# A feed-forward of eight block products per block pair rewritten as two phases over matrix quarters with seven

## The chip, the cores and the metric

The kernel runs on one core of one Trainium2 chip. The metric is the device time of an execution in microseconds (us). The engines are named as in the profile: PE is TensorE, DVE VectorE, ACT ScalarE, POOL GpSimd, SP SyncE, which here only issues transfers.

## The reference

One layer over 1024 tokens of 1024 values, in fp32. Four branches mix the tokens and end in `w_out`; the feed-forward with a hidden width of 4096 follows. Only its end matters here:

```python
hl = hl + ml[2] * yl                                   # yl = (sum of gated branches) @ w_out
bl = modulate(rms_norm(hl, norm_g[i, 1]), ml[3], ml[4])
hl = hl + ml[5] * jnp.square(jax.nn.relu(bl @ w1)) @ w2
return rms_norm(hl, final_g)
```

## The kernel before

Activations lie transposed in SBUF: 128 values by tokens, eight such rows `k` or `d` of values, and two halves of 512 tokens. To keep fp32 accuracy every operand of a large product is split in two: `split` (L72) lets ACT copy it to a rounded high part and DVE subtract that from the original for the low part. `mm3` (L76) then makes three matmuls of 128x512 for a block: high by high, low by high, high by low.

In the stage before, w_out, `hl` is made for each half and row `d` from 24 matmuls, an eviction by DVE that adds the input, ACT's square and POOL's sum of squares (`sum_sq`, L221). At the end of a half the sums are taken by PE against ones, and `second_norm` (L1356) makes the reciprocal root in twelve small DVE steps, broadcasts it by PE (`bcast_rows`, L254) and writes the two parts `blh`, `bll` of the normalised tokens.

The feed-forward runs over 16 blocks of 256 hidden values. For each, `ff1` (L1397) makes the hidden values of one half of the tokens: 8 rows x 3 matmuls for each of two 128-wide chunks, ReLU and square on ACT, and a split into `hh` and `hlw`. `ff2` (L1425) multiplies them by the block's two rows of `w_ff2` and adds each of the eight results to `hl` on DVE. Weights come in transfers of 512 KB on SP's queue (`load_w`, `load_chunk`) and are split in halves of 1024. The second half's `second_norm` is a generator that is advanced between the first block's products. `last_norm` (L1435) takes the final norm into the last block, the second half of tokens in two pieces of 256. The order on each engine is made by a scheduler from the program order and the buffers.

## Time and profile before

| | us |
|---|---|
| median of three runs (lowest, highest) | 1675.32 (1674.51, 1675.99) |
| the profiled execution | 1672.36 |
| its span, first to last instruction | 1670.6 |
| PE busy | 1636.5 (98%) |
| DVE, ACT, POOL busy | 935.9, 552.0, 185.7 |

The span is what one profiled execution of the core shows; 1.76 us of its own time lie around it. Busy time of an engine says how full it is, not what waits for it.

### The profile page before, as it was taken

The page shows a single profiled execution, that of the slowest core. Times are in us where ns is not written, and L with a number is a line of the kernel's source. Part 1 is how long each engine was busy: PE and PEld are TensorE (multiplying, and loading weights), DVE is VectorE, ACT ScalarE, POOL GpSimd, SP SyncE. Part 2 cuts the span into 40 slices and gives each one's busy share as a digit, 9 for nine tenths or more (in the row PEclk, how much of TensorE's full clock was granted, in tenths as well). Part 3 has the DMA queues.
Part 4 walks back from the last instruction along what each step waited for, and adds up shares of the span by engine and source line. Part 5 has one row for each costly group of instructions (what it writes and reads, how often), then busy time and mean ns, then how long its engine had stood idle before and what let it go on. Part 6 is the DMA issues. An engine that isn't in the chain of part 4 may idle for free.

```text
span 1670.6 us, 21735 instructions
## 1 busy us (share of the span) xinstructions
PE 1636.5 (98%) x8464; PEld 1352.7 (81%) x8464; DVE 935.9 (56%) x1913; ACT 552.0 (33%) x897; POOL 185.7 (11%) x281
## 2 busy tenths in 40 slices
PE   8999999999999999999999999999999999999996
PEld 7787878887787787788888888888888888888885
DVE  5797787966556736744446554444444444444455
ACT  3433123222246535623233432222222222222234
POOL 2311102113211212110012200000000000000003
PEclk7999999999999999999999999999999999999997
DMA  8332204425322333143334311111111111111102
GB/s 301 117 99 75 59 27 139 122 86 172 130 86 89 130 107 116 69 157 96 96 109 133 124 51 51 51 51 51 43 46 51 51 51 51 51 51 51 39 1 101
DMA packets 59703, 145.27 MB, mean 87 GB/s; under 512 B 15953, under 2 KB 23713, under 8 KB 59601
## 3 DMA queue, kind: packets, MB, share of 16 engines
q1 hardware_dynamic: 35264, 93.09, 16.7%
q0 software_dynamic: 14688, 47.69, 9.0%
q10 hardware_dynamic: 9648, 3.12, 0.8%
q8 instruction: 66, 1.08, 0.3%
q14 instruction: 37, 0.30, 0.1%
HBM read 126.33 MB, written 17.53 MB: 86 GB/s over the span
## 4 chain that ended last, share of the span: by engine, by line
PE 87%; DVE 6%; DMA 2%; ACT 2%; issue 2%; POOL 0%; SPq 0%; DVEq 0%; ACTq 0%; POOLq 0%
PE mm L77 25%; PE mm L78 25%; PE mm L79 25%; PE po L1189 2%; PE pt L1172 1%; DMA x<-in_xT 1%; PE sc L1146 1%; PE sc L1147 1%; PE mm L736 0%; PE mm L738 0%; PE mm L737 0%; DVE wlo L63 0%; PE pn L235 0%; DMA mraw<-in_ada 0%; PE pt L1176 0%
## 5 line engine op out<-in xcount | busy, mean ns | idle before, releaser
L77 PE MATMUL mm<-alh,whi 128*128 128x512 f32 x704 | 280.1, 398 | 0.4 <-DVE gsg L63 0.4
L79 PE MATMUL mm<-alh,wlo 128*128 128x512 f32 x704 | 276.7, 393 | 0.0
L78 PE MATMUL mm<-all,whi 128*128 128x512 f32 x704 | 276.6, 393 | 0.0
L70 DVE SCALAR_TENSOR_TENSOR hl<-mm,modl,hl 128x512 f32<-128x512 f32 (+1 forms) x264 | 189.9, 732 | 102.9 <-PE mm L79 102.8
L78 PE MATMUL mm<-hlw,w2h 128*128 128x512 f32 (+1 forms) x528 | 202.6, 384 | 1.7 <-DVE hlw L63 1.7
L79 PE MATMUL mm<-hh,w2l 128*128 128x512 f32 (+1 forms) x528 | 202.8, 385 | 0.0
L63 DVE TENSOR_TENSOR wlo<-raw,whi 128x1024 fp32r<-128x1024 f32 x92 | 112.9, 1228 | 159.1 <-ACT whi L73 158.9
L77 PE MATMUL mm<-hh,w2h 128*128 128x512 f32 (+1 forms) x528 | 201.6, 385 | 0.0
L78 PE MATMUL mm<-bll,whi 128*128 128x512 f32 x512 | 199.8, 390 | 0.0
L77 PE MATMUL mm<-blh,whi 128*128 128x512 f32 x512 | 199.6, 390 | 0.0
L79 PE MATMUL mm<-blh,wlo 128*128 128x512 f32 x512 | 199.5, 390 | 0.0
L73 ACT ACTIVATE whi<-raw 128x1024 fp32r<-128x1024 f32 x92 | 97.3, 1059 | 261.2 <-PE mm L78 249.8
L77 PEld LDWEIGHTS mm<-alh,whi 128*128 128x128 f32 x704 | 132.4, 188 | 28.6 <-issue 2.6
L79 PEld LDWEIGHTS mm<-alh,wlo 128*128 128x128 f32 x704 | 132.5, 188 | 27.9 <-issue 1.2
L78 PEld LDWEIGHTS mm<-all,whi 128*128 128x128 f32 x704 | 132.6, 188 | 27.0 <-issue 1.5
L63 DVE TENSOR_TENSOR hlw<-r,hh 128x512 fp32r<-128x512 f32 x64 | 48.3, 754 | 169.3 <-ACT hh L73 169.3
L78 PEld LDWEIGHTS mm<-hlw,w2h 128*128 128x128 f32 x528 | 99.9, 189 | 22.0 <-DVE hlw L63 2.3
L73 ACT ACTIVATE w2h<-raw 128x1024 fp32r<-128x1024 f32 x32 | 33.9, 1059 | 252.6 <-PE mm L78 250.9
L77 PEld LDWEIGHTS mm<-hh,w2h 128*128 128x128 f32 x528 | 99.4, 189 | 20.4 <-ACT hh L73 1.3
L79 PEld LDWEIGHTS mm<-hh,w2l 128*128 128x128 f32 x528 | 99.9, 189 | 19.5
L77 PEld LDWEIGHTS mm<-blh,whi 128*128 128x128 f32 x512 | 96.1, 188 | 20.1
L79 PEld LDWEIGHTS mm<-blh,wlo 128*128 128x128 f32 x512 | 96.1, 188 | 19.9
(448 smaller groups left out, 2575.0 us busy)
## 6 DMA issues: line engine op xcount, KB each, us to landing
raw<-in_w_ff SPq DMA_DIRECT2D x64, 512.0 KB, 3.3
raw<-in_w_in SPq DMA_DIRECT2D x52, 512.0 KB, 3.6
mraw<-in_ada POOLq DMA_DIRECT2D x64, 256.0 KB, 3.4
pmd<-pm POOLq DMA_DIRECT2D x16, 512.0 KB, 3.7
pm<-pmd POOLq DMA_DIRECT2D x16, 512.0 KB, 3.9
raw<-in_w_out SPq DMA_DIRECT2D x16, 512.0 KB, 3.7
ad<-in_ada SPq DMA_DIRECT2D x10, 512.0 KB, 8.4
x<-in_xT SPq DMA_DIRECT2D x8, 512.0 KB, 7.2
```

What stands on the lines that cost most here:

```text
L63: V.tensor_tensor(out=o, in0=x, in1=y, op=op)
L70: V.scalar_tensor_tensor(out=o, in0=x, scalar=s, in1=y, op0=op0, op1=op1)
L73: S.activation(hi, src, AF.Copy)
L77: T.matmul(acc, w[0], x[0], start=start, stop=False)
L78: T.matmul(acc, w[0], x[1], start=False, stop=False)
L79: T.matmul(acc, w[1], x[0], start=False, stop=stop)
L1146: T.matmul(o, q1[h][:, qs], kk, start=True, stop=False)
L1147: T.matmul(o, q2z[h], kk, start=False, stop=True)
L1172: T.transpose(pa[:, b * 128 : (b + 1) * 128], e[:, b * 128 : (b + 1) * 128], ident)
L1189: T.matmul(o[64 * h : 64 * h + 64], vtok[:kp, vt, head * 64 : head * 64 + 64], pts[h][:kp, b], start=(b == 0), stop=(b == nblk - 1), tile_ ...
```

## The change

The two matrices of the feed-forward and its tokens are taken in quarters: halves of the inner rows and halves of the tokens or outer rows. A product of two 2x2 block matrices is then made of seven block products of sums and differences of the blocks instead of eight (Strassen's scheme in Winograd's form). A *visit* `u` is one pair of 128-wide output blocks: 16 visits of the first matrix, 16 of the second. In a visit, product `j` (0 to 6) is 12 matmuls of 128x512 between the split weight combination `ah`, `al` and one of seven token operands `xo[j]`, each of a high and a low part of 128x4x512.

- The weights come as quarters of 256 KB (tag `raw`, 6 buffers). POOL makes `s1` to `s4` from them in each visit; every combination that is multiplied is split by ACT and DVE, three products ahead (`LOOK`).
- The products of a visit accumulate in three banks X, Y, Z. `after1` evicts them and makes seven combinations of the hidden values with ACT, DVE and POOL, and writes each to memory (`hopd`, SP's queue). `after2` adds the results of the second matrix to `hl`, four of seven through ACT and POOL, three by DVE.
- Behind visits 15, 19, 23 and 27, `refill` loads the next four rows of each combination from memory and splits them into the same single `xo[j]`: 28 loads, 28 ACT copies, 28 DVE subtractions each time.
- The first eight visits (`PRO`) are divided: their products 0 and 1 come first, sixteen in all, while the second norm ends and `first_operands` builds `xo[2]` to `xo[6]`. What they leave goes through memory (`m1d`, `hopd[0]`), and the five others of each visit come after.
- `hl` goes to memory in the w_out stage (`hld`) and is loaded again at the 17th product. The last norm takes the second half of tokens in one piece.

```diff
-        def ff1(w1, half, more=()):
-            xs = slice(half * 512, half * 512 + 512)
-            hh = fp.tile([128, 2, 512], F32R, tag=f"hh{half}", name=f"hh{half}", bufs=2)
-            hlw = fp.tile([128, 2, 512], F32R, tag=f"hlw{half}", name=f"hlw{half}", bufs=2)
-            for c in range(2):
-                acc = ps_mm()
-                w = w1[c]
-                for k in range(NK):
-                    mm3(acc, (w[0][:, k], w[1][:, k]), (blh[:, k, xs], bll[:, k, xs]), k == 0, k == NK - 1)
-                r = fp.tile([128, 512], F32, tag="r", name="r", bufs=3)
-                S.activation(r, acc, AF.Relu)
-                S.activation(r, r, AF.Square)
-                split(hh[:, c], hlw[:, c], r)
-                if more:
-                    next(more, END)
-                    next(more, END)
-            return hh, hlw
...
+                stt(hl[:, d, xs], acc, modl[0][:, d : d + 1], xin, ALU.mult, ALU.add)
+                nc.sync.dma_start(hld[:, d, xs], hl[:, d, xs])
+                sum_sq(dp, ss, hl[:, d, xs], d, 512, G)
...
+        for u in range(0, PRO, 2):
+            visits((u, u + 1), (0, 1))
+        for u in range(PRO):
+            visits((u,), (2, 3, 4, 5, 6))
+        for u in range(PRO, 28):
+            visits((u,), range(7))
+        for js in ((0, 1, 2, 4, 6), (3, 5)):
+            for u in (28, 30):
+                visits((u, u + 1), js)
+        def fetch(v):
+            if v["raw"] is None:
+                u = v["u"]
+                v["raw"] = []
+                for c in range(1 if v["js"] == (0, 1) else 2):
+                    src = a["w_ff1"][2 * u + c] if u < 16 else a["w_ff2"][u - 16, c]
+                    for k in range(2):
+                        raw = t_("raw", 6)
+                        nc.sync.dma_start(raw, src[:, 512 * k : 512 * k + 512])
+                        v["raw"].append(raw)
...
+        def prep(n):
+            v, j = steps[n]
+            fetch(v)
+            js = v["js"]
+            q11, q12, *rest = v["raw"]
+            if rest and not v["sums"]:
+                q21, q22 = rest
+                s1, s2 = t_("s", 4, "s1"), t_("s", 4, "s2")
+                G.tensor_tensor(out=s1, in0=q21, in1=q22, op=ALU.add)
+                G.tensor_tensor(out=s2, in0=s1, in1=q11, op=ALU.subtract)
+                v["sums"] = {2: s2, 3: s1, 6: q22}
+                if 4 in js:
+                    s3 = v["sums"][4] = t_("s", 4, "s3")
+                    G.tensor_tensor(out=s3, in0=q11, in1=q21, op=ALU.subtract)
+                if 5 in js:
+                    s4 = v["sums"][5] = t_("s", 4, "s4")
+                    G.tensor_tensor(out=s4, in0=q12, in1=s2, op=ALU.subtract)
+            src = q11 if j == 0 else q12 if j == 1 else v["sums"][j]
+            hi = fp.tile([128, 512], F32R, tag="ah", name="ah", bufs=4)
+            lo = fp.tile([128, 512], F32R, tag="al", name="al", bufs=4)
+            split(hi, lo, src)
+            aops[n] = (hi, lo)
...
+        def product(n, bank, first):
+            j = steps[n][1]
+            hi, lo = aops.pop(n)
+            xh, xl = xo[j]
+            for k in range(4):
+                ks = slice(k * 128, k * 128 + 128)
+                T.matmul(bank, hi[:, ks], xh[:, k], start=first and k == 0, stop=False, skip_group_check=True)
+                T.matmul(bank, hi[:, ks], xl[:, k], start=False, stop=False, skip_group_check=True)
+                T.matmul(bank, lo[:, ks], xh[:, k], start=False, stop=k == 3, skip_group_check=True)
...
+        def operand(j, k, src, eng=None):
+            xh, xl = xo[j]
+            S.activation(xh[:, k], src, AF.Copy)
+            (eng or V).tensor_tensor(out=xl[:, k], in0=src, in1=xh[:, k].bitcast(F32), op=ALU.subtract)
...
+        def after1(u, j, c, pro):
+            if j == 0:
+                c["m1"] = t_("m", 5)
+                S.activation(c["m1"], c["Z" if pro else "X"], AF.Copy)
+                if pro:
+                    nc.sync.dma_start(m1d[u], c["m1"])
+            elif j == 1:
+                h = c["h11"] = hid()
+                if pro:
+                    square(h, c["Z"])
+                else:
+                    tt(h, c["Z"], c["m1"], ALU.add)
+                    square_v(h)
+                save(0, u, h)
+            elif j in (2, 4):
+                m = c["u2" if j == 2 else "u3"] = t_("m", 5)
+                if pro:
+                    tt(m, c["X"], c["m1"], ALU.add)
+                else:
+                    S.activation(m, c["X"], AF.Copy)
+                if j == 4:
+                    h = c["h22"] = hid()
+                    G.tensor_tensor(out=h, in0=m, in1=c["m5"], op=ALU.add)
+                    square(h, h)
+                    save(5, u, h)
+            elif j == 3:
+                c["m5"] = t_("m", 5)
+                S.activation(c["m5"], c["Y"], AF.Copy)
+            elif j == 5:
+                h = hid()
+                tt(h, c["Y"], c["u2"], ALU.add)
+                square_v(h)
+                t3 = hid()
+                G.tensor_tensor(out=t3, in0=c["h22"], in1=h, op=ALU.subtract)
+                save(4, u, t3)
+                G.tensor_tensor(out=h, in0=h, in1=c["h11"], op=ALU.subtract)
+                save(3, u, h)
+                t2 = c["t2"] = hid()
+                tt(t2, c["h22"], h, ALU.subtract)
+                save(2, u, t2)
+            else:
+                h = hid()
+                if pro:
+                    tt(h, c["X"], c["m1"], ALU.add)
+                    square_v(h)
+                else:
+                    square(h, c["X"])
+                save(1, u, h)
+                t4 = hid()
+                tt(t4, h, c["t2"], ALU.subtract)
+                save(6, u, t4)
...
+        def after2(u, j, c):
+            d = 2 * (u % 4)
+            s1, s2 = modl[3][:, d : d + 1], modl[3][:, d + 1 : d + 2]
+            o11, o12, o21, o22 = (box["hl"][:, e, xs] for e in (d, d + 1) for xs in (T1s, T2s))
+            def part(bank, s, o, eng=G):
+                m = t_("m", 5)
+                S.activation(m, bank, AF.Copy, scale=s)
+                eng.tensor_tensor(out=o, in0=o, in1=m, op=ALU.add)
+            def whole(bank, s, o):
+                stt(o, bank, s, o, ALU.mult, ALU.add)
+            if j == 0:
+                part(c["X"], s1, o11)
+            elif j == 1:
+                whole(c["Z"], s1, o11)
+                if u >= 28:
+                    norm_part(d, 0)
+            elif j == 2:
+                part(c["X"], s1, o12)
+            elif j == 3:
+                part(c["Y"], s2, o22, V if u >= 28 else G)
...
+        def refill(j, kb):
+            xo[j] = x_op(P_xa if j < 2 else xbp, j)
+            for q in range(4):
+                t = hid()
+                nc.sync.dma_start(t, hopd[j][4 * kb + q])
+                operand(j, q, t)
...
+        LOOK, AHEAD = 3, 8
+        box = {}
+        live = {}
+        norm2 = second_norm(fp, ss, 1)
+        first = first_operands()
+        next(norm2)
+        for n in range(LOOK):
+            prep(n)
+        for n, (v, j) in enumerate(steps):
+            u, pro = v["u"], v["pro"]
+            for w, _ in steps[n : n + AHEAD]:
+                fetch(w)
+            if n + LOOK < len(steps):
+                prep(n + LOOK)
+            if n < 2 * PRO:
+                for g in (norm2, norm2, norm2) if n < 4 else (first,):
+                    next(g, END)
+            elif n == 2 * PRO:
+                for _ in first:
                     pass
-                continue
-            h0 = ff1(w1, 0)
-            if b < NB - 1:
-                h1 = ff1(w1, 1)
-                w2 = ff2_weights(b)
-                for half, h in ((0, h0), (1, h1)):
-                    for _ in ff2(w2, h, half * 512, 512):
-                        pass
+                box["hl"] = P_hl.tile([128, NK, L], F32, tag="hl", name="hl")
+                for d in range(NK):
+                    nc.sync.dma_start(box["hl"][:, d], hld[:, d])
+                S.activation(one, onec, AF.Sqrt)
+            c = live.setdefault(u, {})
+            nxt = steps[n + 1] if n + 1 < len(steps) else (v, j)
+            if u < PRO and j == 2 or n + 1 == 2 * PRO:
+                w = u + 1 if j == 2 else 0
+                if w < PRO:
+                    m = live[w]["m1"] = t_("m", 5, "m1")
+                    nc.sync.dma_start(m, m1d[w])
+            if pro and j == 3:
+                c["h11"] = hid()
+                nc.sync.dma_start(c["h11"], hopd[0][u])
+            bank = "Z" if j == 1 or (pro and j == 0) else "Y" if j in (3, 5) else "X"
+            fresh = j in (0, 3) or (j == 1 and not pro) or (j == 2 and pro)
+            if fresh:
+                c[bank] = ps_mm()
+            product(n, c[bank], fresh)
+            if u < 16:
+                after1(u, j, c, pro)
             else:
-                w2 = ff2_weights(b)
-                last_norm(w2, h0, 0, 512, False)
-                h1 = ff1(w1, 1)
-                last_norm(w2, h1, 512, 256, False)
-                last_norm(w2, h1, 768, 256, True)
+                after2(u, j, c)
+            if u in (15, 19, 23, 27) and j <= 6:
+                refill(j, (u - 15) // 4)
```

On PE, where w_out ends, there was before (`pn` is the bank of sums and broadcasts, `mm` one of products):

```order
L79 MATMUL mm<-mh,wlo 128x512
L235 MATMUL pn<-ones,sqa 128x1 x4
L77 MATMUL mm<-blh,whi 128x512
L78 MATMUL mm<-bll,whi 128x512
L79 MATMUL mm<-blh,wlo 128x512
```

The same place now:

```order
L81 MATMUL mm<-mh,wlo 128x512
L241 MATMUL pn<-ones,sqa 128x1 x4
L241 MATMUL pn<-ones,sq 128x1 x4
L264 MATMUL pn<-dg,ones 128x128 x3
L1491 MATMUL mm<-xh_7710,ah 128x512
L264 MATMUL pn<-dg,ones 128x128
L1492 MATMUL mm<-xl_7711,ah 128x512
```

The second half's remaining sums and its broadcast, which stood among the first products, now stand ahead of them. On POOL nothing stood in the feed-forward before its last norm:

```order
L1384 DMA xin<-in_xT 128x512
L231 TENSOR_TENSOR sqa<-sqa,sq 128x512 x2
L1454 TENSOR_TENSOR hl<-hl,rs 128x2x512 x4
L1454 TENSOR_TENSOR hl<-hl,rs 128x2x256 x5
```

In one of the visits of five products it now has (L1552 makes `h22`, L1563 `t3`, L1565 `h`−`h11`; `s1` to `s4` belong to the visits behind):

```order
L1470 TENSOR_TENSOR s1_9490<-raw_9394,raw_9396 128x512
L1552 TENSOR_TENSOR t_9385<-m_9383,m_9357 128x512
L1471 TENSOR_TENSOR s2_9491<-s1_9490,raw_9390 128x512
L1475 TENSOR_TENSOR s3_9494<-raw_9390,raw_9394 128x512
L1563 TENSOR_TENSOR t_9417<-t_9385,t_9414 128x512
L1565 TENSOR_TENSOR t_9414<-t_9414,t_9342 128x512
L1478 TENSOR_TENSOR s4_9496<-raw_9392,s2_9491 128x512
```

Two weight sums stand between `h22` and what is made from it. On DVE, in a block of the feed-forward, there was before:

```order
L63 TENSOR_TENSOR wlo_9552<-raw_9549,whi_9551 128x1024
L70 SCALAR_TENSOR_TENSOR hl_7697<-mm_9415,modl3_78,hl_7697 128x512
L63 TENSOR_TENSOR w2l_9682<-raw_9679,w2h_9681 128x1024
L63 TENSOR_TENSOR hlw1_9342<-r_9398,hh1_9341 128x512
L70 SCALAR_TENSOR_TENSOR hl_7697<-mm_9423,modl3_78,hl_7697 128x512
```

Now, at the refill behind visit 19 (`al` are splits of weights, `xl0` and `xl1` the low parts of refilled operands):

```order
L65 TENSOR_TENSOR al_11863<-s1_11793,ah_11862 128x512
L65 TENSOR_TENSOR al_11901<-s3_11797,ah_11900 128x512
L1498 TENSOR_TENSOR xl0_11883<-t_11884,xh0_11882 128x512
L1498 TENSOR_TENSOR xl0_11883<-t_11888,xh0_11882 128x512
L1498 TENSOR_TENSOR xl0_11883<-t_11892,xh0_11882 128x512
L1498 TENSOR_TENSOR xl0_11883<-t_11896,xh0_11882 128x512
L72 SCALAR_TENSOR_TENSOR hl_8918<-mm_11904,modl3_78,hl_8918 128x512
L1498 TENSOR_TENSOR xl1_11919<-t_11920,xh1_11918 128x512
```

Four subtractions for each operand now stand between the splits of the weights.

## Rows read from the trace of the kernel before

**Rows 1.** The page: span, busy time by engine, the chain that ended last.

```profile
span 1670.6 us, 21735 instructions
PE 1636.5 (98%) x8464; PEld 1352.7 (81%) x8464; DVE 935.9 (56%) x1913; ACT 552.0 (33%) x897; POOL 185.7 (11%) x281
...
PE 87%; DVE 6%; DMA 2%; ACT 2%; issue 2%; POOL 0%; SPq 0%; DVEq 0%; ACTq 0%; POOLq 0%
```

**Rows 2.** Table of stretches; the first is the feed-forward.

```profile
core 0: us, PE busy (x) PEld busy (x) DVE busy (x) ACT busy (x) POOL busy (x), PEclk, DMA share, GB/s
943.00:1652.40 709.40, 707.42 (x3169) 585.42 (x3169) 328.81 (x450) 205.24 (x309) 9.88 (x4) 1.00 0.15 49
220.00:230.00 10.00, 7.88 (x37) 5.03 (x36) 10.00 (x27) 1.06 (x1) 0.00 (x0) 0.83 0.00 1
...
1000.00:1200.00 200.00, 200.00 (x882) 165.37 (x882) 88.81 (x112) 53.27 (x76) 0.00 (x0) 1.00 0.15 50
1640.00:1645.00 5.00, 4.18 (x24) 4.18 (x25) 4.25 (x11) 3.08 (x9) 0.22 (x1) 0.71 0.32 120
```

**Rows 3.** Timeline where w_out ends: start, duration, engine, line, operation, [idle before].

```profile
942.16 0.95 PE L235 MATMUL pn<-ones,sqa 128*128 128x1 f32 x8
...
942.36 0.75 DVE L70 SCALAR_TENSOR_TENSOR hl<-mm,modl,xin 128x512 f32<-128x512 f32 x1 [3.30 <-PE mm L79]
...
942.97 0.48 PE L77 MATMUL mm<-blh,whi 128*128 128x512 f32 x1
...
944.66 0.62 ACT L229 ACTIVATE sq<-hl 128x512 f32<-128x512 f32 x1
...
946.00 0.95 PE L235 MATMUL pn<-ones,sq 128*128 128x1 f32 x8
...
950.19 0.16 DVE L70 SCALAR_TENSOR_TENSOR rd_y<-rd_q,rd_y 128x4 f32<-128x4 f32 x1
...
950.82 0.68 PE L258 MATMUL pn<-dg,ones 128*128 128x128 f32 x4
```

**Rows 4.** PE's timeline in the last block, 256 tokens wide.

```profile
1640.82 0.38 PE L78 MATMUL mm<-hlw,w2h 128*128 128x256 f32 x1 [1.74 <-DVE hlw L63]
1641.04 0.28 PE L79 MATMUL mm<-hh,w2l 128*128 128x256 f32 x1
1641.16 0.28 PE L78 MATMUL mm<-hlw,w2h 128*128 128x256 f32 x1
...
1642.35 0.42 PE L77 MATMUL mm<-hh,w2h 128*128 128x256 f32 x1
1642.56 0.41 PE L78 MATMUL mm<-hlw,w2h 128*128 128x256 f32 x1
...
1645.53 0.28 PE L77 MATMUL mm<-hh,w2h 128*128 128x256 f32 x1
```

**Rows 5.** POOL's timeline, in w_out and in the last norm.

```profile
911.36 2.05 POOL L231 TENSOR_TENSOR sqa<-sqa,sq 128x512 f32<-128x512 f32 x1
...
917.70 2.08 POOL L231 TENSOR_TENSOR sqa<-sqa,sq 128x512 f32<-128x512 f32 x1
...
923.02 1.39 POOL L231 TENSOR_TENSOR sqa<-sqa,sq 128x512 f32<-128x512 f32 x1
...
1630.34 9.88 POOL L1454 TENSOR_TENSOR hl<-hl,rs 128x1024 f32<-128x1024 f32 x4 [690.13 <-ACT rs L1447]
...
1662.55 1.27 POOL L1454 TENSOR_TENSOR hl<-hl,rs 128x512 f32<-128x512 f32 x1 [3.07 <-ACT rs L1447]
```

**Rows 6.** DVE's timeline at the same places.

```profile
912.18 1.77 DVE L70 SCALAR_TENSOR_TENSOR bll<-t,modl,blh 128x512 fp32r<-128x512 f32 x1
...
917.39 1.22 DVE L63 TENSOR_TENSOR wlo<-raw,whi 128x1024 fp32r<-128x1024 f32 x1
...
1632.76 2.88 DVE L63 TENSOR_TENSOR hlw<-r,hh 128x512 fp32r<-128x512 f32 x1 [3.68 <-ACT hh L73]
1638.21 2.56 DVE L63 TENSOR_TENSOR hlw<-r,hh 128x512 fp32r<-128x512 f32 x1 [2.56 <-ACT hh L73]
```

**Rows 7.** Groups by line and form, DVE and ACT: xcount | busy us, mean ns | idle before.

```profile
L70 DVE SCALAR_TENSOR_TENSOR hl<-mm,modl,hl 128x512 f32<-128x512 f32 x248 | 182.5, 748 | 102.3 <-PE mm L79 102.2
L63 DVE TENSOR_TENSOR hlw<-r,hh 128x512 fp32r<-128x512 f32 x64 | 48.3, 754 | 169.3 <-ACT hh L73 169.3
L63 DVE TENSOR_TENSOR gwl<-raw,gwh 128x512 fp32r<-128x512 f32 x16 | 11.0, 685 | 0.0
...
L73 ACT ACTIVATE hh<-r 128x512 fp32r<-128x512 f32 x64 | 40.5, 632 | 2.0
L1407 ACT ACTIVATE r<-mm 128x512 f32<-128x512 f32 x64 | 37.6, 588 | 138.1 <-PE mm L79 138.1
```

**Rows 8.** Transfers of 256 KB: queue, count, size, median us from issue to landing.

```profile
raw<-in_wbr SPq DMA_DIRECT2D x16, 256.0 KB, 2.7
...
out<-hl SPq DMA_DIRECT2D x7, 256.0 KB, 2.2
```

**Rows 9.** PE's timeline at the end, behind the last product.

```profile
1652.04 0.28 PE L79 MATMUL mm<-hh,w2l 128*128 128x256 f32 x1
...
1657.28 0.99 PE L235 MATMUL pn<-ones,sqa 128*128 128x1 f32 x4 [3.60 <-DVE sqa L231]
```

More of the change, by code (lines that the diff above doesn't have):

```diff
@@ L44 @@
 PI_PARTS = _parts(TWO_PI, (9, 11, 11))
+PRO = 8
 R_CONV = 2
@@ L105, in tile_backbone @@
     ysd = dram.tile([2, 128, 2, 1024], F32, name="ysd")
+    hld = dram.tile([128, NK, L], F32, name="hld")
+    m1d = dram.tile([PRO, 128, 512], F32, name="m1d")
+    hopd = [dram.tile([16, 128, 512], F32, name=f"hop{j}") for j in range(7)]
     def rsqrt_steps(y, v, q):
@@ new lines, in t_, with hid, visits @@
+        def t_(tag, bufs, name=None):
+            return fp.tile([128, 512], F32, tag=tag, name=name or tag, bufs=bufs)
+        def hid():
+            return t_("t", 7)
+        steps = []
+        def visits(us, js):
+            vs = [dict(u=u, js=js, raw=None, sums=None, pro=u < PRO) for u in us]
+            steps.extend((v, j) for j in js for v in vs)
+        for u in range(0, PRO, 2):
+            visits((u, u + 1), (0, 1))
+        for u in range(PRO):
+            visits((u,), (2, 3, 4, 5, 6))
```

170 lines of the change are left out of this document (97 added, 73 removed).

## The prediction

> **What bounds the kernel now.** I read the page first: TensorE (PE) is busy for 98% of the span and holds 87% of the chain that ended last [rows 1]. Then the table of stretches: from the first to the last product of the feed-forward PE is busy 707.42 of 709.40 us at full clock, and in a quiet stretch 882 matmuls take 200.00 us [rows 2], so 0.2268 us each, back to back. Before, the feed-forward is 3024 such matmuls and 96 half as wide (0.12 us apart, [rows 4]): 697.3 us, and 12 us of anything else. VectorE (DVE) is busy 329 us of it, ACT 205, POOL 10 [rows 2]. So only fewer matmuls, or PE waiting, can move the time here, and three engines have room for more work if it comes in time. The weights are fetched and split well ahead.
>
> **What is removed.** 32 visits x 7 products x 12 matmuls = 2688 matmuls of the old shape, in place of the equivalent of 3072: 609.6 us. Against the whole old stretch of 709.3 us (942.97 to 1652.3, [rows 3, 9]) that leaves **99.7 us** to be eaten by waits.
>
> **Prices of what is added.** Every new operation is a 128x512 one. On DVE, a split's subtraction or a combination costs 0.68, an eviction with an addend 0.75; on ACT a copy 0.63, an eviction 0.59 [rows 7]; a 256 KB transfer lands 2.2 to 2.7 us after its issue [rows 8]. On POOL an addition takes 1.27 when alone [rows 5]; with dispatch I use 1.3.
>
> What decides is whether DVE and POOL can work side by side. Two rows say they often cannot: the subtraction hlw<-r,hh, two operands from SBUF, takes 0.75 in the mean [rows 7], but 2.88 and 2.56 us in the two cases that fell under POOL's four multiplications from 1630.34 to 1640.22 [rows 5, 6]. The second one ends 0.55 us after POOL's last. The other way round, POOL's addition at 917.70 takes 2.08: DVE's wlo runs until 918.61, and from there 1.17 us are left. And bll at 912.18 takes 1.77 in place of 0.75 beside POOL's addition of 911.36 to 913.41. So I count the time of such DVE operations and of POOL's in one sum, as if they shared one engine. Evictions from PSUM stay outside it.
>
> The Trainium skill, "SBUF — State Buffer", section "Who interferes with whom", makes this a rule: a DVE instruction with two SBUF inputs and a GpSimd instruction that reads SBUF exclude each other for the whole instruction. It speaks against this change, which gives POOL 7 or 8 additions in a visit. These rows agree, in single meetings; no row here shows a long contest. Applied with no slip at all, it would add 4.5 to the first products and 12.6 to the refills below: 84 in place of 67, and the time 1660; with every meeting free the first rival would hold.
>
> **Start (+5.5).** Before, the first product runs at 942.97, right behind the sums of the last w_out block, and the second norm's remainder (ACT's square at 944.66, sums at 946.00, rsqrt until 950.35, broadcast at 950.82) hides under products [rows 3]. In the changed order PE has both sums and three of four broadcast matmuls ahead of the first product. With ACT freer: eviction to 943.1, square 943.8, sums 944.9, twelve small DVE steps of 0.2 each 947.3, dg and broadcast 948.4. That is 5.4 us; bounds 4 and 9 (with PE slow afterwards).
>
> **First 16 products, 43.5 us (+5).** The port sum is: DVE 16 splits and 24 norm and operand steps with two SBUF inputs (27 us), POOL 12 operand steps and some 8 weight sums (26 us), 53 us in all. About half of the excess of 9.5 can slide behind them. Bounds 0 and 10.
>
> **Eight visits of five products, 13.6 us each (+20).** Port sum: DVE 5 splits, 2 squares, 2 subtractions at 0.68 (6.1), POOL 7 at 1.3 (9.1): 15.2, so at least 1.6 too long if all of it excludes. The loop that closes on itself is longer: eviction of product 4, then on POOL h22, the two sums that its queue puts between, t3 and h−h11, then t2 on DVE and what DVE has in its queue, the eviction of product 2 of the next visit, and product 4, which accumulates into the bank so read. It is 7.4 us of DVE and PE and five POOL steps: 7.4 + 5 x 1.3 = 13.9 without sharing, and 16.3 with some 2.4 us of DVE's splits in POOL's way. I take 2.5 us a visit, nearer to the loop; bounds 0 and 5.
>
> **Eight visits of seven products (+2).** Port sum 7.5 + 9.1 = 16.6 of 19.05 us; room is left. Bounds 0 and 8.
>
> **Four refills (+10, then 8, 8, 8).** In the steady second phase the port sum is 4.8 + 10.4 = 15.2 of 19.05. A refill adds 28 subtractions, 19.0 us, between the last product of an operand and its next, so within two visits (38.1 us): 30.4 + 19.0 = 49.4. If none of it slid, 11.3 us would be lost each time, and 12.7 at the first, where a visit of the first phase stands ahead. POOL's additions to hl can slip by the five buffers m (6.5 us), which gives some back; against that the operands are single, so each load waits for the last product of its operand, then 2.7 us to land, 0.63 and 0.68 to split, behind which the splits for the next products queue on ACT and DVE: walked by hand that alone costs 3.5 a time, and 5 at the first, where the saves stand ahead of the loads on SP. I take 8, and 10 at the first. Bounds 10 and 70 for the four. Outside the refills the second phase loses nothing: POOL's eight additions take 10.4 of 19.05 us, and if that cover failed DVE would have to take them at 0.68 each, still within the visit.
>
> **Rest.** Sums and broadcasts that PE still has: +2. Tail: before, 18.3 us follow the last product (1652.3 to 1670.6), 5.0 of them until the sums at 1657.28, since the squares' additions ran against POOL [rows 9]. After, 0.75 and 0.63 and a little (2.1) stand there; the last multiplications and stores are of 512 tokens, 1.3 longer: −1.6. The saves of hl on SP stand behind each eviction; the next weight load's buffer comes free later than that, so I put them at 0; if they held up the loads, each costs up to 2.2 us [rows 8], which the 24 products of a block (5.4 us) cover.
>
> **Sum.** 5.5 + 5 + 20 + 2 + 34 + 2 − 1.6 = 66.9 of the 99.7: −32.8. The profiled execution took 1672.36 (span 1670.6 and 1.76 around it), so 1639.6; the median of the runs lies 2.96 above that execution: **1642**.
>
> **Rivals.**
> - *The added work is hidden.* For it: DVE has more than half of this stretch idle, and POOL's first addition beside an idle DVE took 1.39 (923.02). Then the visits of five cost 14.35 (+6), the refills the hand walk's 5 + 3 x 3.5, the first products nothing: losses 27.4, time 1603. Against it: the 2.88 and 2.56.
> - *PE's clock drops at the gaps.* A PE idle of 1.74 us before 1640.82 is followed by matmuls 0.21 apart in place of 0.12 from 1642.35 until 1645.53 [rows 4], at a granted clock of 0.71 over that stretch, and a 2.1 us idle at 220 goes with 0.83 [rows 2]; so such a gap costs about 1.7 us more. Smaller gaps do not show it. If all 8 visits of five, two gaps per refill and three at the start are of that size: 19 x 1.7 = 32, time 1675, no change.
> - *Slower: refills in series.* The loads use t, of which there are seven; a refill takes four, so the next one's loads wait for its subtractions. One refill alone is 2.7 + 0.63 + 4 x 0.68 + POOL between (1.3) = 7.4 against 2.72 of its product. Were they strictly in series, 7 x 4.7 = 33 less some 8 of prepared products = 25 a time, 100 in place of 34: 1708. It decides from 17 us a refill upwards, where the sum is back at 1675. Against it: nearly two refills fit the seven buffers, and the next use is a whole visit away.
>
> **Chances.** My sum 0.52 (1622 to 1660 by its own bounds), hidden 0.25, clock 0.13, series 0.10. About 3.4 us (0.2%) can be told from no change. The clock's rival straddles it: faster 0.83, same 0.04, slower 0.13. The range reaches from the hidden case to the clock's: 1600 to 1676.
>
> **What would show it.** In the profile after: 2688 products spaced 0.2268 where PE doesn't wait; first product 5 to 6 us behind the last of w_out; visits of five at 15 to 17 us, with PE idle released by an eviction of DVE behind POOL; means of POOL's additions above 1.5 and of DVE's splits above 0.8 where both run, and not elsewhere; visits 16, 20, 24 and 28 later than 19.05 us by 8 to 10 together with the one ahead. I am wrong if POOL and DVE overlap without growing, if PE's idle time is spread over the steady visits, or if waits on SP's queue (a raw that lands late) end most of it.

## The result and the profile after

The changed kernel takes **1692.7 us** (four executions, 1689.13 to 1694.16) against 1674.91 (1673.66 to 1675.99) before: a ratio of 1.0103 [1.0085, 1.0122]. It is slower by 1%, where −2% was predicted. The profiled execution is the slowest of the four (1694.16).

The page of the changed kernel, the lines that answer to [rows 1], and the granted clock in 40 slices:

```profile
span 1692.4 us, 22506 instructions
PE 1600.0 (95%) x8032; PEld 1297.0 (77%) x8032; DVE 1058.2 (63%) x2027; ACT 672.2 (40%) x1147; POOL 557.8 (33%) x533
...
PEclk7999999999999999999999999899999999999997
...
PE 62%; DVE 15%; DMA 8%; issue 7%; ACT 4%; POOL 3%; SPq 0%; DVEq 0%; POOLq 0%; ACTq 0%
```

By the prediction's count PE has 384 full matmuls less, 87 us at the old spacing, and it has lost only 36.5 us of busy time. So those that are left cost more each, even before any wait is counted. PE's part of the chain fell from 87% to 62%.

The table of stretches, in this order: the start; the first 16 products; visits 2 to 6; visits 8 to 14; visits 15 to 17 around the first refill; the last 28 products:

```profile
core 0: us, PE busy (x) PEld busy (x) DVE busy (x) ACT busy (x) POOL busy (x), PEclk, DMA share, GB/s
946.00:953.57 7.57, 3.94 (x23) 3.54 (x22) 3.88 (x19) 3.80 (x6) 0.00 (x0) 0.65 0.65 230
953.57:1009.81 56.24, 48.38 (x196) 37.80 (x196) 44.96 (x51) 32.60 (x59) 26.43 (x17) 0.96 0.52 169
1044.36:1138.00 93.64, 79.85 (x302) 62.66 (x301) 43.96 (x65) 23.59 (x41) 48.76 (x35) 0.89 0.51 168
1156.48:1293.12 136.64, 136.64 (x589) 110.80 (x588) 79.59 (x94) 59.38 (x104) 70.64 (x50) 1.00 0.42 148
1293.12:1365.56 72.44, 63.48 (x254) 48.67 (x253) 54.23 (x63) 37.71 (x68) 38.46 (x26) 0.95 0.65 215
1577.42:1675.46 98.04, 89.29 (x362) 70.94 (x361) 65.82 (x77) 50.80 (x83) 58.91 (x37) 0.91 0.33 109
```

The fourth row is the surprise. Seven visits of 84 matmuls run without one wait and at full clock, yet they take 136.64 us: 19.52 a visit, 0.2324 a matmul, where [rows 2] had 0.2268. The other rows lose through PE's idle time and through the clock. (PE's busy time counts a slowed matmul as busy, so the stretch minus PE's busy time understates the loss.)

What ended PE's waits from 950 to 1680 us (total, times, longest; one of the two in the fifth line lies behind the last product):

```profile
PE mm L1491 <- DVE m L65: 19.5, 7, 3.2
PE mm L1491 <- ACT m L1590: 11.8, 10, 2.8
PE mm L1493 <- DVE al L65: 11.3, 7, 4.4
PE mm L1491 <- ACT m L1533: 7.9, 4, 3.3
PE pn L264 <- DVE dg L69: 4.6, 2, 2.9
...
PE mm L1492 <- DVE xl L1498: 2.2, 3, 0.8
```

The sum of the prediction, term by term. "Measured" is a stretch's time from first product to first product, less its matmuls x 0.2268; the spacing's part is taken out of each and stands in its own line.

| term | predicted | measured |
|---|---|---|
| spacing of the 2688 matmuls | 0 | 15.0 |
| start | 5.5 | 6.8 |
| first 16 products | 5 | 11.6 |
| eight visits of five | 20 | 35.1 |
| visits 8 to 14 | 2 | 0 |
| four refills | 34 (10, 8, 8, 8) | 39.1 (13.9, 6.2, 8.0, 11.0) |
| rest (sums and broadcasts on PE, end) | 2 | 11.2 |
| tail | −1.6 | −1.4 |
| sum | 66.9 | 117.4 |

The last 28 products and visit 27 lose 22.2 together; 11.2 of that is lost without a last refill too (e3 below), which is the line "rest". 117.4 − 99.7 gives +17.7. Another 3.8 of the span's 21.8 lie ahead of the feed-forward, which the sum left out: w_out's last product ends at 946.0, before at 942.2. The longest wait that is new is one near 411 us, in a stage whose operations are the same (changed kernel, then the one before):

```profile
411.41 0.50 PE L79 MATMUL mm<-sg_yh,gwh 128*128 128x512 f32 x1 [3.53 <-ACT gsg L1267]
```

```profile
408.08 0.50 PE L77 MATMUL mm<-sg_yh,gwh 128*128 128x512 f32 x1 [0.46 <-ACT gsg L1261]
```

It is hardly chance: the wait is 2.7 to 3.5 us in all 17 profiles of changed kernels (of the kernel before there is one profile). The change also gives the pool of the weights, which the stages ahead use, another way of handing on its buffers (`reuse_waits="tile"`, L86; the section on the change does not name it). No run tells whether that is the reason. In the kernels below the first product starts anywhere from 950.1 to 955.9. The last 0.3 is rounding and crumbs.

### The profile page after: what moved, and what is told of

The parts are those of the page before. It is cut to its first block, busy times and chain, and to the rows that moved or that the text cites. A ratio compares the mean times of both kernels' runs of the same rounds, so it can differ in the third digit from the quotient of the medians.

```text
span 1692.4 us, 22506 instructions
## 1 busy us (share of the span) xinstructions
PE 1600.0 (95%) x8032; PEld 1297.0 (77%) x8032; DVE 1058.2 (63%) x2027; ACT 672.2 (40%) x1147; POOL 557.8 (33%) x533
## 4 chain that ended last, share of the span: by engine, by line
PE 62%; DVE 15%; DMA 8%; issue 7%; ACT 4%; POOL 3%; SPq 0%; DVEq 0%; POOLq 0%; ACTq 0%
PE mm L79 10%; PE mm L80 10%; PE mm L81 9%; PE mm L1491 8%; PE mm L1492 8%; PE mm L1493 8%; DMA t<-hop 3%; PE po L1195 2%; DVE xl L1498 2%; DMA raw<-in_w_ff 2%; DVE al L65 1%; DMA mraw<-in_ada 1%; ACT xh L1497 1%; PE pt L1178 1%; DVE t L65 1%
## 5 line engine op out<-in xcount | busy, mean ns | idle before, releaser
L1491 PE MATMUL mm<-xh,ah 128*128 128x512 f32 x896 | 365.8, 408 | 42.9 <-DVE m L65 19.5
L1493 PE MATMUL mm<-xh,al 128*128 128x512 f32 x896 | 364.3, 407 | 11.3 <-DVE al L65 11.3
L1492 PE MATMUL mm<-xl,ah 128*128 128x512 f32 x896 | 363.6, 406 | 2.2 <-DVE xl L1498 2.2
L1491 PEld LDWEIGHTS mm<-xh,ah 128*128 128x128 f32 x896 | 175.0, 195 | 94.6 <-issue 17.0
L1493 PEld LDWEIGHTS mm<-xh,al 128*128 128x128 f32 x896 | 174.4, 195 | 56.4 <-DVE al L65 15.3
L1492 PEld LDWEIGHTS mm<-xl,ah 128*128 128x128 f32 x896 | 174.1, 194 | 44.0 <-DVE xl L1498 3.5
L65 DVE TENSOR_TENSOR al<-s,ah 128x512 fp32r<-128x512 f32 x128 | 118.6, 930 | 55.3 <-ACT ah L75 55.3
L65 DVE TENSOR_TENSOR al<-raw,ah 128x512 fp32r<-128x512 f32 x96 | 89.9, 943 | 60.8 <-ACT ah L75 56.6
L1591 POOL TENSOR_TENSOR hl<-hl,m 128x512 f32<-128x512 f32 x60 | 91.5, 1527 | 82.7 <-ACT m L1590 82.4
L1498 DVE TENSOR_TENSOR xl<-t,xh 128x512 fp32r<-128x512 f32 x120 | 105.3, 918 | 7.4 <-ACT xh L1497 7.3
```

The costliest lines, as they stand in the source:

```text
L65: V.tensor_tensor(out=o, in0=x, in1=y, op=op)
L1491: T.matmul(bank, hi[:, ks], xh[:, k], start=first and k == 0, stop=False, skip_group_check=True)
L1492: T.matmul(bank, hi[:, ks], xl[:, k], start=False, stop=False, skip_group_check=True)
L1493: T.matmul(bank, lo[:, ks], xh[:, k], start=False, stop=k == 3, skip_group_check=True)
L1498: (eng or V).tensor_tensor(out=xl[:, k], in0=src, in1=xh[:, k].bitcast(F32), op=ALU.subtract)
L1591: eng.tensor_tensor(out=o, in0=o, in1=m, op=ALU.add)
```

## The experiments

Each ratio is to the kernel before, run beside it on the same chip; "−x" is against 1692.7. The runs were made on several chips, on which the medians of the kernel before lie within 0.9 us. Where no ratio is given, the kernel was run once: executions of one kernel spread over 3 to 17 us, so such a total decides nothing, and the reading rests on the stretches. Diffs are against the changed kernel.

### Why are the matmuls 0.2324 apart?

The form of the instructions differs from the old one in several ways (which operand comes first, which bank accumulates how long, the order of high and low). The rival is the place of the operands in SBUF.

**e1_forms** gives one form each to ten of the visits 9 to 25, and so leaves out or alters part of those products:

```diff
+                if u == 9:
+                    st = k == 0
+                    sk = {}
...
+                elif u == 11:
+                    kk = 0
+                elif u == 12:
+                    ks = slice(0, 128)
+                elif u == 13:
+                    seq = [(hi, xh), (lo, xh), (hi, xl)]
```

> The products of the changed kernel run 0.2324 us apart in undisturbed visits (19.52 us for 84), those of w_out in the same execution 0.2268. Thirteen visits get one altered form each: 9 ends its accumulation group with each product and opens a new one, 10 opens one with each product, 11 always the first rows of the operand, 12 always the first columns of the weights, 13 the order high-low-high of weights, 14 no low weights, 18 no low operand, 21 low by low, 22 a group for each matmul, 25 one pair of operands three times. The parts left out or repeated make the result another one. Theory 1, the spacing comes from what the matmuls read or how they accumulate: one of these visits falls to 0.2268, so 19.05 us. Theory 2, it comes from something outside the matmuls, such as what the other engines and the queues do in this stretch: all stay at 0.232 to 0.234.

1695.39. Every altered visit stays at 232.4 to 233.4 ns a matmul. None of these forms matters.

**f1_low_weights** opens a pool for `ah` and `al` ahead of the token operands, which puts `xo[2]` to `xo[6]` 16 KB higher, and changes nothing else. By the program's allocation the weights then lie at bytes 18144 to 34528 of a partition instead of 112480 to 128864:

```diff
+    P_wt = ExitStack()
+    wtp = P_wt.enter_context(pool("p_wt", reuse_waits="tile"))
...
-            hi = fp.tile([128, 512], F32R, tag="ah", name="ah", bufs=4)
-            lo = fp.tile([128, 512], F32R, tag="al", name="al", bufs=4)
+            hi = wtp.tile([128, 512], F32R, tag="ah", name="ah", bufs=4)
+            lo = wtp.tile([128, 512], F32R, tag="al", name="al", bufs=4)
```

> The split weights ah and al lie at the low end of SBUF (addresses 18144 to 34528 of a partition) in place of 112480 to 128864, the operands xo[2] to xo[6] 16 KB higher; nothing else is changed. The altered forms of the products left their spacing at 0.2324, so neither accumulation nor which rows they read sets it. Theory 1, where the weights lie does (before, all weights lay below 89856): undisturbed visits fall from 19.52 to 19.05 us and the kernel is 12 to 15 us faster. Theory 2, it is something else in this stretch: 19.52, no difference.

1684.35, ratio 1.0056 [1.0034, 1.0078], −8.3. The same 130 us of undisturbed visits, first in the changed kernel, then with low weights:

```profile
1160.00:1290.00 130.00, 130.00 (x561) 105.43 (x560) 77.51 (x90) 56.19 (x98) 66.86 (x47) 1.00 0.43 152
```

```profile
1160.00:1290.00 130.00, 130.00 (x575) 107.64 (x574) 78.39 (x93) 58.97 (x103) 67.80 (x47) 1.00 0.43 154
```

575 matmuls in place of 561, as before the change; an undisturbed visit takes 19.04. About half of the 15 us is kept. Where PE waits for other engines the quicker products gain nothing: the eight visits of five take 146.6 us here and 146.7 in the changed kernel, the first 16 products 56.2 in both.

**i2_ah_low** moves `ah` alone, **i3_alternate** both for every second product (`wp = fp if n % 2 else wtp`):

> Only the high parts ah of the weights lie low (18144 to 26336), al stays high. Theory 1, each weight load from the high place costs its matmul some 17 ns: two of three matmuls are quick, visits of 19.05 + 28 x 0.017 = 19.5 at most, if the slow one alone loses all, or 19.2 if it loses its own share of 5.6 ns a matmul. Theory 2, the operands' place (8 KB higher) did it: 19.05 as with both moved.

> Even products take their weights from the low place, odd ones from the high one; the operands lie 8 KB higher than in the changed kernel for all. Theory 1, the weights' place sets the spacing: 0.2268 in even products, 0.232 to 0.234 in odd ones, after a few matmuls of each. Theory 2, it is the operands' place or the layout as a whole: one spacing for all.

With `ah` low the spacing is 0.2311 in the mean and the total 1687.14. Only the step between the two matmuls that both take `ah` is quick (226.7 ns); the steps on either side of `al`'s matmul take 232.7 and 234.0. Alternating gives 1686.56 and two patterns. The eleven spacings of products 65 (high) and 66 (low), in ns, worked out from the start times:

```
65 high  241 233 230 232 228 230 233 241 232 231 232
66 low   236 224 231 236 228 233 230 227 227 226 227
```

The low product comes down to 227 after some seven matmuls, the high one never does. So the place of the stationary operand (the weights, which PE loads ahead of each matmul) sets the spacing, within one kernel and one stretch. Why its start is slow, and at which address the border lies, stays open.

### What closes the loop of the visits of five?

The prediction's loop went from the eviction of product 4 through POOL and DVE back to product 4. The trace of the changed kernel shows the same end, but another link (visits 5 and 6; start, duration, engine, line):

```profile
1108.02 1.65 POOL L1478 TENSOR_TENSOR s<-raw,s 128x512 f32<-128x512 f32 x1 [2.00 <-DVE al L65]
...
1109.29 0.77 PE L1491 MATMUL mm<-xh,ah 128*128 128x512 f32 x1 [2.83 <-DVE m L65]
...
1110.14 0.68 DVE L65 TENSOR_TENSOR al<-raw,ah 128x512 fp32r<-128x512 f32 x1
...
1110.24 0.32 SPq L1527 DMA_DIRECT2D hop<-t  x1
...
1110.65 0.89 SPq L1456 DMA_DIRECT2D raw<-in_w_ff  x2
...
1115.15 1.29 POOL L1470 TENSOR_TENSOR s<-raw 128x512 f32<-128x512 f32 x1 [5.49 <-DMA raw<-in_w_ff]
...
1116.40 1.30 POOL L1552 TENSOR_TENSOR t<-m 128x512 f32<-128x512 f32 x1
...
1123.36 1.29 POOL L1565 TENSOR_TENSOR t<-t 128x512 f32<-128x512 f32 x1
...
1124.68 0.69 DVE L65 TENSOR_TENSOR t<-t 128x512 f32<-128x512 f32 x1 [3.81 <-POOL t L1565]
...
1127.09 0.68 DVE L65 TENSOR_TENSOR m<-mm,m 128x512 f32<-128x512 f32 x1
...
1127.92 0.48 PE L1491 MATMUL mm<-xh,ah 128*128 128x512 f32 x1 [3.18 <-DVE m L65]
```

A visit needs four `raw` buffers and there are six. POOL's last weight sum of visit 5, `s4` (L1478), has done with a quarter at 1109.67. SP issues the load into its buffer at 1110.65, behind the save at 1110.24, as the first of two; the second goes into the buffer that the split at 1110.14 frees. POOL's first sum of the next visit starts when the first load has landed, 4.5 us after the issue, and has then waited 5.49 us, with h22 (1116.40), the other sums and everything up to DVE's `t2` (1124.68) queued behind. So POOL's own last sum closes the loop, through the buffer and the transfer. Then DVE's eviction of the next visit's product 2 is late, and PE waits 3.18 for the bank. By the order in which the buffers are handed out, a seventh lets this quarter follow the read of `s3` instead, 6 us earlier.

**g1_one_load** leaves the loads of these visits out but for the first one's (visits 1 to 7 use the quarters of visit 0); **h3_raw7** takes one buffer from `t` for `raw`:

```diff
-                        raw = t_("raw", 6)
+                        raw = t_("raw", 7)
...
-            return t_("t", 7)
+            return t_("t", 6)
```

> Left out: the weight loads of visits 1 to 7 for their products 2 to 6; the quarters of visit 0 serve all eight, so the result is another one. Theory 1 (the loop through the weights' buffers and loads): POOL's first sum waits for no load, visits 1 to 6 fall from 18.4 to 16.5 us or less. Theory 2 (POOL's and DVE's sum): they stay at 17.5 or more.

> Seven buffers for raw weight quarters in place of six, six for t in place of seven. Theory 1, the loop of the visits of five runs through the freeing of a raw buffer, the load into it and the first sum: with one buffer more it has one quarter's freedom, visits 1 to 6 fall from 18.4 to 17 us or less (leaving the loads out gave 15.7). Theory 2, all four quarters are freed together too late for one more buffer to matter: 18 or more. The refills, which load into t, lose 1 to 3 us each with one buffer fewer by either.

Both give visits 2 to 7 of 15.70 to 15.76 us, in place of 17.6 to 20.0, with one wait of 1.49 to 1.55 each and the clock at 1.00. Visit 1 gains nothing (19.1 and 20.1 us, for 18.5), and with one buffer fewer for `t` the first products take 59.55 us for 56.24 (59.4 in h4 and i1 below). Totals: 1669.21 and 1678.93. In h3, POOL in the same operations, and PE behind them:

```profile
1058.04 1.30 POOL L1470 TENSOR_TENSOR s<-raw 128x512 f32<-128x512 f32 x1 [1.89 <-DVE al L65]
1059.67 1.61 POOL L1552 TENSOR_TENSOR t<-m 128x512 f32<-128x512 f32 x1 [0.33 <-issue]
1061.24 1.30 POOL L1471 TENSOR_TENSOR s<-s,raw 128x512 f32<-128x512 f32 x1
...
1071.51 0.47 PE L1491 MATMUL mm<-xh,ah 128*128 128x512 f32 x1 [1.50 <-DVE m L65]
```

The first sum no longer waits for a transfer. What is left ends as the loop that the prediction described, at DVE's eviction, and is near its size: 13.6 + 2.5 predicted, 15.7 measured. That it is this loop link by link was not tested.

Two edits were meant for the other links. **e2_pro_act** shortens the eviction of product 2, with ACT's copy freeing the bank and DVE adding `m1` later; **f3_prep_late** writes POOL's sums behind the visit's own additions in the program:

```diff
-                if pro:
+                if pro and j == 4:
...
+                    if pro:
+                        tt(m, m, c["m1"], ALU.add)
```

```diff
+            late = pro and n >= 2 * PRO
+            if n + LOOK < len(steps) and not late:
...
+            if late and n + LOOK < len(steps):
+                prep(n + LOOK)
```

> In the eight visits of five products the bank of product 2 is copied out by ACT, and DVE adds m1 afterwards, off the bank. Theory 1, PE waits before product 4 only because that eviction stands in DVE's queue behind t2, which waits for POOL: the seven waits of 1.8 to 3.2 us and the half clock after each (1.7 us of time each) go, visits fall from 18.5 to 14 us, and the whole kernel is 30 to 35 us faster (about 1660). Theory 2, the sum of POOL's time and DVE's bounds the visits whatever evicts (7 additions of 1.27 and 10 operations of 0.68, 15.7 us): visits stay at 16 or above, with another wait in place of the old, and the gain is 18 us at most.

> In the visits of five products the weight sums and splits of a later product are written behind the product and its eviction, not ahead; POOL's queue then has h22 ahead of s1, and s2, s3 behind t3 and h-h11. Theory 1, the visit's loop runs through the weights (s1 waits for a quarter that is loaded into a buffer which DVE frees late, and h22 stands behind s1 on POOL): visits fall from 18.4 to 15 to 16.5 us, 16 to 25 us faster. Theory 2, it is the sum of POOL's and DVE's time that bounds: order does not matter, 17.5 us or more, under 8 us faster.

e2: 1689.05, ratio 1.0087 [1.0066, 1.0109], −3.6; the wait moves to product 6 (2.11 each) and to `al`, and that gain lies within the noise. f3: 1693.74, 1.0113 [1.0087, 1.0138], visits of 17.1 to 20.2. But f3 did not do what was expected of it: the scheduler put POOL's operations back in the old order, `s1` still ahead of h22 and still waiting for the load.

```profile
1115.13 1.29 POOL L1470 TENSOR_TENSOR s<-raw 128x512 f32<-128x512 f32 x1 [5.50 <-DMA raw<-in_w_ff]
1116.38 1.74 POOL L1552 TENSOR_TENSOR t<-m 128x512 f32<-128x512 f32 x1
1118.08 1.30 POOL L1471 TENSOR_TENSOR s<-s,raw 128x512 f32<-128x512 f32 x1
```

So f3 says nothing on the order. While the load closes the loop, the shorter eviction is worth little; what another order would be worth stays open.

### What makes the refills dear?

**e3_no_refill** leaves the refills behind visits 19, 23 and 27 out (the operands of 15 stay); **e4_no_pool_add** leaves POOL's additions of results to `hl` out (60 in all, four in most visits); **f2_dve_results** gives them to DVE, in one operation from the bank:

```diff
-            if u in (15, 19, 23, 27) and j <= 6:
+            if u == 15 and j <= 6:
```

```diff
-                eng.tensor_tensor(out=o, in0=o, in1=m, op=ALU.add)
+                if eng is V:
+                    V.tensor_tensor(out=o, in0=o, in1=m, op=ALU.add)
```

```diff
-                m = t_("m", 5)
-                S.activation(m, bank, AF.Copy, scale=s)
-                eng.tensor_tensor(out=o, in0=o, in1=m, op=ALU.add)
+                stt(o, bank, s, o, ALU.mult, ALU.add)
```

> Left out: the refills behind visits 19, 23 and 27 (84 loads, copies and subtractions); the operands of visit 16 serve to the end, so the result is another one. Theory 1, the refills cost what visits 19, 20, 23, 24, 27 and 28/29 lost (6, 8 and some 11 us with the half clock): 22 to 27 us faster, the waits on al and on ACT's m gone there, and only the wait before the last products left. Theory 2, these waits come from the steady work of the visits and the pairing of the last four: under 10 us.

> Left out: POOL's additions of three results to hl in each visit of the second phase but the last four's (and two there), so the result is another one; ACT's evictions stay. Theory 1, POOL's additions stretch DVE's subtractions (0.93 in the mean for 0.68 alone) and this is what delays the splits in the refills: DVE's mean there falls to 0.75 or less and visits 16 to 29 lose 10 to 20 us less. Theory 2, the refills wait for their loads and the single operands: the waits stay, gain under 5 us.

> In the second phase all seven results of a visit are added to hl by DVE straight from the bank (0.75 us each) in place of four by ACT and POOL. Theory 1, POOL's additions in DVE's way were what made the refills late (leaving them out gave 19 us), and an eviction from the bank does not meet POOL: POOL's share is gone for 4 x 0.75 more on DVE a visit, 10 to 19 us faster. Theory 2, DVE is the bound in a refill whoever runs beside it (42 subtractions of 0.68 and 14 evictions of 0.75 are 39 us in two visits of 38.1): what POOL gives back DVE takes, under 6 us.

e3: 1669.2, ratio 0.9972 [0.9957, 0.9988], −23.5. Visits 18 to 27 wait for nothing (195.20 us are ten of 19.52):

```profile
1368.54:1563.74 195.20, 195.20 (x842) 158.25 (x841) 69.54 (x100) 67.41 (x111) 103.75 (x81) 1.00 0.17 53
```

e4: 1673.32, 1.0001 [0.9983, 1.0019], −19.4. DVE's subtractions of the refills from 1300 to 1660 us (count | busy us, mean ns | idle before), first in the changed kernel, then in e4:

```profile
L1498 DVE TENSOR_TENSOR xl<-t,xh 128x512 fp32r<-128x512 f32 x112 | 97.3, 912 | 6.0 <-ACT xh L1497 5.9
...
L1591 POOL TENSOR_TENSOR hl<-hl,m 128x512 f32<-128x512 f32 x60 | 91.5, 1527 | 82.7 <-ACT m L1590 82.4
```

```profile
L1498 DVE TENSOR_TENSOR xl<-t,xh 128x512 fp32r<-128x512 f32 x112 | 78.8, 747 | 5.4 <-ACT xh L1497 5.2
```

So POOL's additions stretch each subtraction from 747 to 912 ns in the mean. Without them the second and third refill cost 2.0 and 2.3, and visit 27 with the last 28 products 11.3 for 22.2, as without a last refill; the first, where visit 15 of the first phase stands ahead, still costs 12.3. f2: 1685.98, 1.0065 [1.0043, 1.0088], −6.7 (the intervals just touch), and all of it at the end (visit 27 and the last products lose 12.5 for 22.2); the other three refills cost 12.3, 7.9 and 8.1, now in waits for DVE's own evictions `hl`. The work has left POOL, and DVE's queue is as long.

The last refill in the changed kernel, where these meet (start, duration, engine, line; `x4` are four in a row):

```profile
1584.12 3.47 DVE L1498 TENSOR_TENSOR xl<-t,xh 128x512 fp32r<-128x512 f32 x2
...
1585.30 3.42 POOL L1591 TENSOR_TENSOR hl<-hl,m 128x512 f32<-128x512 f32 x2
...
1588.18 2.90 DVE L1498 TENSOR_TENSOR xl<-t,xh 128x512 fp32r<-128x512 f32 x4
1591.00 0.68 DVE L65 TENSOR_TENSOR al<-raw,ah 128x512 fp32r<-128x512 f32 x1
...
1591.73 0.80 PE L1493 MATMUL mm<-xh,al 128*128 128x512 f32 x1 [4.42 <-DVE al L65]
```

Two subtractions beside two additions of POOL take 3.47, four alone 2.90; the split `al` that PE waits for stands behind all six, and an eviction, in DVE's queue.

DVE's subtractions hold PE in a second way. PE's waits for ACT (`ACT m L1590` above, 11.8 us) are as long as those for `al` (11.3). In the second refill, from the timelines of ACT and PE, and then from SP's waits between 1393 and 1425 us (total, times, longest):

```profile
1413.58 0.63 ACT L1497 ACTIVATE xh<-t 128x512 fp32r<-128x512 f32 x1 [1.33 <-DMA t<-hop]
1414.11 0.67 ACT L1590 ACTIVATE m<-mm,modl 128x512 f32<-128x512 f32 x1
...
1414.84 0.50 PE L1491 MATMUL mm<-xh,ah 128*128 128x512 f32 x1 [1.74 <-ACT m L1590]
```

```profile
SPq L1624 <- DVE xl L1498: 13.1, 21, 2.3
```

ACT's eviction stands behind a copy that waits for its load, and the loads wait for DVE's subtractions to free a `t`.

### Together

| kernel | edits | us | ratio |
|---|---|---|---|
| h1_low_dve_act | f1, f2, e2 | 1673.64 | 0.9990 [0.9975, 1.0005] |
| h2_low_dve_pro6 | f1, f2, `PRO = 6` | 1671.81 | 0.9981 [0.9967, 0.9996] |
| h4_low_raw7 | f1, f2, h3 | 1669.00 | 0.9968 [0.9955, 0.9982] |
| i1_best | f1, f2, e2, h3 | 1663.97 | 0.9939 [0.9918, 0.9960] |
| i4_best_m1 | i1, and DVE evicts `m1` | 1664.36 | 0.9947 [0.9927, 0.9967] |

> Three edits together: the split weights low in SBUF, the second phase's results by DVE alone, product 2 of the visits of five copied out by ACT. Theory 1, they act at three places and add up: undisturbed visits 19.05 us, refills as with the second edit, visits of five near 18: 8 to 15, 7 and 4 us less than 1692.7, so 1667 to 1674, level with the kernel before or a little faster. Theory 2, PE only waits elsewhere once its products are quicker: more than half of it is lost again, 1680 or more.

> The split weights low, the second phase's results by DVE alone, and six divided visits in place of eight (12 products cover the second norm and the operands, 33 us for 43). Theory 1, a divided visit costs 4.4 to 4.9 us through its trip by memory and its loop, so two fewer give 9, and the operands, done 47 us after the first product, make the first products wait some 5 to 10 longer: 0 to 5 us less than without it, 1668 to 1678. Theory 2, the first products' cover was not the limit, nothing is waited for longer: 9 us less, 1662 to 1668.

> The split weights low, the second phase's results by DVE alone, seven buffers for raw quarters and six for t. Theory 1: 1692.7 less 8 to 15, 7, and 8 to 10 for visits of five at 17 us, plus 4 to 8 for later refills: 1665 to 1678. Theory 2 (the buffer does nothing in the visits of five): 1676 to 1686.

> The three edits of the fastest so far (split weights low, results of the second phase by DVE, seven buffers for raw quarters) and product 2 of the visits of five copied out by ACT. Theory 1, with the loads out of the loop only the eviction in DVE's queue holds product 4 (1.5 to 1.8 us each, some with half clock behind): visits of five fall from 15.4 to 17.3 to 14 to 15, 8 to 14 us less than 1669: 1655 to 1661. Theory 2, the next wait (POOL and DVE together, 15.9 us) takes its place as it did with six buffers: 1665 to 1670.

> As i1_best, and in the first sixteen products DVE copies m1 out of the bank in place of ACT. Theory 1, PE waits there because ACT's copy stands behind operand copies that wait for POOL and DVE: the waits of 2.2, 0.9, 1.2 and 3.3 us shrink, 3 to 8 us less than i1_best. Theory 2, DVE's queue holds the same operand steps: the wait only changes its name, within 3 us of i1_best.

With the load out of the loop e2's eviction looks worth 5 us (h4 to i1; their intervals overlap a little), less than the 8 to 14 expected. In the profile of i1, the slowest of its eight executions (1671.46), visits of five take 14.5 to 19.7 and those of seven 19.04. It beats both kernels, the one before by 0.6% and the changed one by 1.6% (0.9939 / 1.0103). h2 buys two visits of seven with four early products less; the first products then lose 16.0 and visit 1 takes 22.4. No run of f1 and f2 alone stands beside it, so whether six are better than eight stays open. i4 only renames the first products' wait: 8.78 us for `DVE m`, where i1 had 8.83 for `ACT m`. What delays the first products was not settled beyond that: of their 56.24 us DVE is busy for 44.96, ACT for 32.60 and POOL for 26.43 (second stretch above).

## Why the prediction was wrong

**What held.** PE is the bound and a product less is a gain where nothing else changes. The places of the waits were as named: visits of five, by DVE's eviction behind POOL; refills; the first products. The start (6.8 for 5.5), the tail (−1.4 for −1.6) and the visits of seven (0 for 2) came out. So did the long sharing of DVE and POOL: by the rule of the Trainium skill's page "SBUF — State Buffer", section "Who interferes with whom", two such operations exclude each other. The runs agree: 912 against 747 ns, and in single meetings 1.7 to 1.8 us on DVE and 1.6 to 1.8 on POOL against 0.68 and 1.29 alone.

**Step 1, the spacing (0, measured 15.0).** "2688 matmuls of the old shape … 609.6 us" took the old spacing for a property of the shape. It belongs to the place of the weights too, which the new pools moved up. f1 and i3 show it. This term was missing from the sum and from its bounds.

**Step 2, the visits of five (20, measured 35.1).** The loop was walked through PE, DVE and POOL; the six `raw` buffers and the transfer's landing were left out, although the prediction itself had listed "a raw that lands late" among what would refute it. The loads in this loop take 4.2 to 4.4 us to land, where 2.2 to 2.7 had been read. With that link broken (h3) visits 2 to 7 lose 2.1 each, near the 2.5 of the sum; with it, visits 1 to 7 lose 4.0 to 6.4. (The expectation of f3 has a buffer that DVE frees late; it is POOL's last sum that frees it.)

**Step 3, the clock (13 in 100, and not in the sum).** The rival came true beside the likeliest case, instead of in its place. In the feed-forward 103 matmuls follow one another at 0.427, the lower of the two clock levels; against 0.2324 that loses 20 us. They are part of the measured terms: a visit of five with a wait of 2.83 takes 18.33 at a clock of 0.91, while h3's wait of 1.5 leaves it at 1.00. Waits and clock had been priced as alternatives; the longer waits bring the clock with them.

**Step 4, the refills and the rest (34 and 2, measured 39.1 and 11.2).** The refills' mechanism and the size of their sum were nearly right: e3 takes them away and gains, e4 shows POOL in DVE's way. One by one they cost 13.9, 6.2, 8.0 and 11.0 for 10, 8, 8 and 8, so that the sum came so near is in part luck. The rest was mis-sized. The sums and broadcasts of the last norm fall among the last products from 1642.5 to 1652.6 us, where "+2" had counted PE's work alone: with the wait for DVE's `sqa` (1.06) and the slow clock between them they cost 7.4. A wait of 2.64 for ACT at 1668.2, behind the last norm's copies, brings the lower clock once more and costs 4.5. e3, without that refill, has both (5.3 and 5.9).

```profile
1642.48 1.02 PE L241 MATMUL pn<-ones,sqa 128*128 128x1 f32 x8 [1.06 <-DVE sqa L237]
...
1668.22 0.59 PE L1491 MATMUL mm<-xh,ah 128*128 128x512 f32 x1 [2.64 <-ACT m L1590]
```

**Step 5, the first products (5, measured 11.6).** Four waits for ACT's eviction `m1` (2.44, 0.95, 1.16, 3.31), which stands in ACT's queue behind operand copies. The prediction summed the work of DVE and POOL and not the order in ACT's queue; i4 shows that the engine's name is not the cause, and what is stays open.

The series rival (25 a refill) did not come true: 6.2 to 13.9. Its link is there all the same: the loads wait for a free `t` (13.1 us in the second refill).

Ahead of the feed-forward the sum took the time of before for granted; the 3.8 us there are a term that it put at nothing, and their cause is open.

## What to carry to other kernels

When a change takes work from the bound engine, walk every loop that is to run faster through its buffers and transfers as well as through its engines, and count buffers against one turn's need. Where new waits appear, price the clock with each wait that is as long as those that brought it down in the traces (here half of the gaps of 1.75 to 3.5 us), not as a separate case. When an edit reorders a program that a scheduler orders again, read the order in the new trace before the time. And a matmul's spacing read from a trace holds for the operands' places as well as their shapes: after moving pools, read it again.

## What the runs showed of the hardware

- The spacing of split matmuls of 128x512 at full clock was 0.2268 us with weights at or below byte 89856 of a partition (before, f1) and 0.2324 at 112480 to 128864, with each of the seven moving operands (231.7 to 232.9 ns), two of which lie in a pool opened from the other side (`side="right"`). At the lower clock it was 0.427 in either place.
- A count over the profiles of all 17 changed kernels, of the products of the feed-forward: of 215 gaps of 0.75 to 1.75 us between two matmuls, 7 were followed by matmuls at the lower clock; of 190 gaps of 1.75 to 3.5, 103; of 64 longer ones, 60. (A gap is the distance of two starts less 0.2324, and counts as followed when four of the next 22 matmuls, up to the next long gap, are 0.39 to 0.47 apart.) Which of the middle ones are followed stays open: in e3, waits near 2.8 us come both with and without.
